# Sums of squares asked for later: the norms between the stages of a one-core encoder layer, and its last norm

## The chip, the cores and the metric

The kernel is one program on one core of a Trainium2 chip. The metric is the device time of one execution in microseconds (us). The core's engines are named as the profile names them: PE (TensorE, matrix products; PEld is its loading of weights), DVE (VectorE), ACT (ScalarE), POOL (GpSimd) and SP (SyncE, whose queue issues most of the loads from HBM). Each engine works through its own instructions in order and waits on semaphores for what the others produce.

## The reference

One layer of a streaming encoder on 1024 prompt frames and 32 sample frames, 1056 tokens in all, of 1024 channels. Each sub-layer stands between two norms, one of its input and one of its output:

```
def rms_norm(x, g):
    xf = x.astype(jnp.float32)
    y = xf * lax.rsqrt(jnp.mean(xf * xf, axis=-1, keepdims=True) + EPS) * g.astype(jnp.float32)
    return y.astype(x.dtype)
...
    mix = (jax.nn.sigmoid(ga) * (oa @ w_br_a) + jax.nn.sigmoid(gb) * (ob @ w_br_b)) @ w_out
    x = x + rms_norm(mix, g_post_mix)
    f, conv_new = conv_ffn(rms_norm(x, g_pre_ffn), conv_s0, w_up, conv_w, conv_b, w_down)
    x = x + rms_norm(f, g_post_ffn)
    gate = jax.nn.sigmoid(rms_norm(x, g_pre_ple) @ w_ple_gate)
    x = x + rms_norm(gate * (pe @ w_ple), g_post_ple)
```

`conv_ffn` is a product with `w_up` (1024 to 2 x 2816), a causal convolution of width 3 over one half of it, a gelu, a product of the two halves, and a product with `w_down` (2816 to 1024). The change touches the norms behind `w_out`, in front of `w_up`, behind `w_down`, in front of `w_ple_gate`, and the last one.

## The kernel before

**Layout and products.** Channels lie on the 128 partitions, in 8 rows of 128; tokens lie along the free dimension. A value in fp32 is kept as a high half (rounded to fp32r by ACT) and a low half (value less high half, by DVE or POOL), and a product is three matmuls: high by high, weight high by low half, weight low by high half. In most of the program the tokens are cut into three parts of 352; in the last stages into a part of 528 ("one"), one of 528 ("two"), and "two" again into 264 ("three") and 264 ("four"). A "pair" is two of the 8 rows.

**What a norm needs.** The squares of the 8 rows are made by ACT, pair by pair, and added up on DVE into an accumulator with two rows; DVE folds the two rows into one, ACT and DVE cut it into a high half h and a low half l, and PE sums it over the partitions by two matmuls with a matrix of ones (two per 264 columns). That is what is called "the sums" here. ACT then takes Ln and Exp of it (behind a load of its table), DVE does one Newton step in three instructions, and the inverse norm is there.

**The order of the work.** PE, DVE and ACT run in an order written out by hand: the code is written in the order in which each engine is to run it, and a generator that makes one norm is advanced step by step between the products. POOL's instructions and the order in which SP issues the loads are chosen by a scheduler that simulates the kernel.

**The up stage.** `norm_steps` (L1099 to L1166) is the generator for one part of 352 tokens. Its steps are: total of the out product's squares; first sums, inverse norm; four joins (scale a pair by channel and token, L1130, add the residual, L1144, with the square of the pair before ahead of it); last square; total; nothing; second sums, inverse norm; four steps that scale a pair again, spill it to the buffer d_hn and make its high and low half (L1159, L1166): the operand of `w_up`. The third part's steps are laid between the products of `up_plain` (L1288): 18 products of 24 matmuls (128 x 352), the table UP_STEPS saying how many steps come after each of the first nine. The sums are L1112 and L1113. Behind these products comes the first unit of a Strassen scheme, `up_first`: its operands are read back from d_hn and differenced on DVE (`quarter_first`, L1334 to L1338, with halves L1329 and L1330), and its weights are differenced too (L1370, halves L1376 and L1377).

**The down stage.** 28 units of 66 matmuls (128 x 264; L1728) accumulate the product with `w_down`. After unit u the program issues, in this order: the split of the weights of unit u+1 (`split_weights`: high halves on ACT, L1656, low halves from u = 19 on POOL, L1657), the additions that take unit u-1 out of PSUM (`evac`), and what a table puts into slot u: squares (`h_square`, L1781, their additions L1789 and L1791), fold and halves (L1796, L1798, L1799), joins (L1839, with the store of y by POOL, L1840), operands of the gate product (`operand`, L1843). The table MID puts the sums (L1807) into the middle of a unit: behind the matmuls of index k of it, six matmuls to an index.

**The gate stage and the tail.** 24 tiles follow (L1728 too), eight for part one, eight for three, eight for four, in a planned order; the table `sched` hangs work behind each. 16 transfers reload gate weights on SP's queue during it (L1989, L1990), and two transfers (`y_load`, L2075) read back part four of y. The last norm of part three has the name f3, that of part four g4: `gains` (L2071) scales a pair by its channel factors on ACT, `final` scales a pair by channel and token on DVE (L1834) and adds it to y by a transfer. Behind the last tile come the sigmoid of the last row, the last sums (L2193), Ln and Exp (L1817, L1818), the Newton step (L1819 to L1821), and four times a product and an addition (L2200, L2201) with a store.

Of the kernel before, what the change touches and what calls it, by code (L numbers as in the profile page):

```python
# [14 lines left out]
AF = mybir.ActivationFunctionType  # L15
# [85 lines left out]
OUT_STEPS = (1, 1, 2, 2, 2, 1, 1, 2)  # L101
UP_STEPS = (1, 1, 2, 2, 2, 1, 1, 2, 3)
DOWN_DVE = (0, 1, 2, 3, 4, 5)
# [3 lines left out]
def emit(tc, a):  # L107
# [992 lines left out]
    def norm_steps(tmp, c, z, acc, g, resid, keep, g_next, dst, spill=None):  # L1100
# [39 lines left out]
        for i in range(KT // 2):  # L1140
            if i:
                squares(tmp, acc2, i - 1, zs[i - 1])
            times(i, g, rs)
            ve.tensor_tensor(zs[i], zs[i], res[i], op=ALU.add)  # L1144
            if len(res) < KT // 2:
                load(len(res))
            po.dma_start(both(keep, i), zs[i])
            yield
# [694 lines left out]
    def operand(i, s, rs, dst):  # L1843
        zz = scaled(i, s, G_PRE_PLE, rs)
        ac.activation(dst[0], zz, AF.Copy)
        ve.tensor_tensor(dst[1], zz, dst[0], op=ALU.subtract)

# [59 lines left out]
    for i, u in enumerate((21, 22, 22, 23)):  # L1907
        at(u, n_join, "r1", i, one)
        at(u, h_square, "a2", i, one)
    at(24, n_total, "r2", "a2")  # L1910
# [3 lines left out]
    for j in range(3):  # L1914
        at(25 + j, h_square, "a3", j, two)
    MID = {21: (0, lambda: n_sum("r1")), 25: (3, lambda: n_sum("r2"))}

# [226 lines left out]
    on(19, g_begin, "g4", 3, four)  # L2144
    on(20, gains, 1, four)
    on(20, final, "f1", 3, one)
    on(21, gains, 2, four)
    on(21, n_inv, "f3")
    on(21, g_sig, "g4", 0)
    on(21, g_pair, "g4", 0, four)  # L2150
    on(22, gains, 0, four)
    on(16, y_load, 0)
# [13 lines left out]
    def g_first():  # L2166
# [4 lines left out]
        settle(acc)  # L2171

    on(22, g_first)
    on(22, final, "f3", 0, three)
    for g, (part, n) in enumerate(plan):
# [16 lines left out]
    for i, t in enumerate([kv[x][:, j] for x in ("g4", "s7") for j in range(2)]):  # L2192
        pe.matmul(ps, onesM, t, start=(i == 0), stop=(i == 3))  # L2193
    ac.activation(z[:, 7, four], z[:, 7, four], AF.Copy, scale=col(G_POST_PLE + 7))
    for i in range(1, 4):
        final("f3", i, three)
    rs = inverse(ps, False)
    for i in range(4):
        zz = z[:, 2 * i : 2 * i + 2, four]
        ve.tensor_tensor(zz, zz, rs.unsqueeze(1).to_broadcast([P, 2, HC]), op=ALU.mult)  # L2200
        ve.tensor_tensor(zz, zz, kv["y", i], op=ALU.add)  # L2201
        (dma, ac)[i % 2].dma_start(rows2(a["y"], i, four), zz)
# [89 lines left out]
```

## Time and profile before

| | us |
|---|---|
| median of 3 runs | 1921.74 |
| lowest and highest of them | 1918.62, 1922.12 |
| the profiled execution's own time | 1919.71 |
| its span, first to last instruction | 1918.0 |
| PE busy in it | 1886.7 (98%) |
| DVE busy | 1260.8 (66%) |
| ACT busy | 907.9 (47%) |
| POOL busy | 458.5 (24%) |

The mean granted clock of TensorE was 0.995. Of the profiled execution's own time, 1.71 us lie outside the span. Where the change lies: the products of `up_plain`, with the third part's norm among them, run from about 1107 to 1183 us of the span, `up_first` begins there, the down units run from 1577 to 1805, the gate tiles from 1805 to 1901.5, the tail from there to 1918.

How the rows are to be read: a row of the timeline has the start, the duration, the engine, the line, the operation, out <- in, the shape and the count of instructions that were taken together, and, in brackets, how long the engine was idle before and what released it. The recorded durations of matmuls overlap: two that follow each other at full rate start 0.12 us apart with 264 columns and 0.16 us apart with 352.

### The profile page before, as it was taken

Reading aid. Unit: us, or ns where it says so; the run is one execution under the profiler, and the core shown is the slowest. Engines: PE = TensorE matmul, PEld = TensorE weight load, DVE = VectorE, ACT = ScalarE, POOL = GpSimd, SP = SyncE. Lnnn points to the kernel's source line nnn. Section 1 sums busy time; section 2 is a strip of 40 time slices with the busy share of each in tenths; the row PEclk is TensorE's granted clock in tenths of the full one; section 3 lists DMA queues with packets and bytes.
Section 4 is the critical chain, followed back from the end, with each engine's and each line's share of the span. In section 5 each row is a group of like instructions: output and inputs, shape, how many; then the busy total and the mean of one; then the engine's idle time right before and its main releaser. Section 6 shows DMA issues by size and latency. Waiting matters only on the chain.

```text
span 1918.0 us, 34182 instructions
## 1 busy us (share of the span) xinstructions
PE 1886.7 (98%) x13364; PEld 1855.4 (97%) x13364; DVE 1260.8 (66%) x2521; ACT 907.9 (47%) x1668; POOL 458.5 (24%) x568
## 2 busy tenths in 40 slices
PE   9999999999999999999999999999999999999997
PEld 8999999999999999999999989999999999999996
DVE  6556556458486385775663787977777776546777
ACT  7456455444372452753334454433333344444545
POOL 2312232332232121222220212322222222115312
PEclk9999999999999999999999999999999999999999
DMA  7334346434445322337884446643443448656677
GB/s 273 120 97 136 114 125 161 119 132 123 108 133 141 104 68 74 112 121 261 309 274 143 148 144 219 198 148 126 153 131 131 136 161 299 193 183 200 200 248 152
DMA packets 106733, 307.77 MB, mean 160 GB/s; under 512 B 13188, under 2 KB 35276, under 8 KB 106444
## 3 DMA queue, kind: packets, MB, share of 16 engines
q1 hardware_dynamic: 80444, 217.64, 34.4%
q0 software_dynamic: 25296, 87.04, 15.3%
q8 instruction: 105, 1.72, 0.4%
q10 hardware_dynamic: 832, 0.90, 0.1%
q14 instruction: 56, 0.46, 0.1%
HBM read 217.79 MB, written 107.60 MB: 170 GB/s over the span
## 4 chain that ended last, share of the span: by engine, by line
PE 83%; DVE 10%; ACT 5%; issue 1%; DMA 1%; SPq 0%; ACTq 0%; DVEq 0%
PE mm L225 13%; PE mm L227 13%; PE mm L226 13%; PE c L1728 11%; PE two L1469 6%; PE two L1467 6%; PE two L1468 6%; PE aux L1728 2%; PE one L593 2%; PE one L551 2%; DVE z L1130 1%; PE two L535 1%; PE two L853 1%; PE one L911 1%; PE two L536 1%
## 5 line engine op out<-in xcount | busy, mean ns | idle before, releaser
L225 PE MATMUL mm<-xh,whi 128*128 128x352 f32 (+2 forms) x1248 | 412.3, 330 | 0.0
L227 PE MATMUL mm<-xh,wlo 128*128 128x352 f32 (+2 forms) x1248 | 409.9, 328 | 0.0
L226 PE MATMUL mm<-xl,whi 128*128 128x352 f32 (+2 forms) x1248 | 408.6, 327 | 0.0
L205 POOL TENSOR_TENSOR wlo<-raw,whi 128x512 fp32r<-128x512 f32 x128 | 187.7, 1470 | 661.3 <-ACT whi L204 657.4
L225 PEld LDWEIGHTS mm<-xh,whi 128*128 128x128 f32 x1248 | 235.2, 188 | 2.1 <-DVE ev L455 0.6
L226 PEld LDWEIGHTS mm<-xl,whi 128*128 128x128 f32 x1248 | 235.0, 188 | 1.5 <-issue 0.7
L227 PEld LDWEIGHTS mm<-xh,wlo 128*128 128x128 f32 x1248 | 234.5, 188 | 1.0
L1469 PE MATMUL two<-mh,wlo 128*128 128x264 f32 x576 | 162.8, 284 | 0.0
L1468 PE MATMUL two<-ml,whi 128*128 128x264 f32 x576 | 162.4, 283 | 0.0
L1467 PE MATMUL two<-mh,whi 128*128 128x264 f32 x576 | 161.1, 284 | 0.7 <-ACT whi L1457 0.7
L204 ACT ACTIVATE whi<-raw 128x512 fp32r<-128x512 f32 x136 | 84.2, 626 | 117.4 <-PE mm L226 88.4
L1728 PE MATMUL c<-mh,whi 128*128 128x264 f32 x396 | 112.4, 284 | 0.0
L1728 PE MATMUL c<-mh,wlo 128*128 128x264 f32 x396 | 112.2, 283 | 0.0
L1728 PE MATMUL c<-ml,whi 128*128 128x264 f32 x396 | 112.2, 283 | 0.0
L1468 PEld LDWEIGHTS two<-ml,whi 128*128 128x128 f32 x576 | 108.3, 188 | 0.0
L1469 PEld LDWEIGHTS two<-mh,wlo 128*128 128x128 f32 x576 | 108.3, 188 | 0.0
L1467 PEld LDWEIGHTS two<-mh,whi 128*128 128x128 f32 x576 | 107.3, 188 | 0.9 <-ACT whi L1457 0.9
L455 DVE TENSOR_TENSOR ev<-mm,rstd 128x352 f32<-128x352 f32 x120 | 61.6, 518 | 65.9 <-PE mm L227 65.3
L1457 ACT ACTIVATE whi<-ws 128x512 fp32r<-128x512 f32 x72 | 45.4, 632 | 99.9 <-PE two L1468 68.9
L555 DVE TENSOR_TENSOR pt<-one,pt 128x128 fp32r<-128x128 f32 (+3 forms) x96 | 46.3, 499 | 52.7 <-ACT pt L554 52.5
L225 PE MATMUL mm<-mh,ahi 128*128 128x352 f32 x240 | 78.1, 325 | 0.0
L226 PE MATMUL mm<-ml,ahi 128*128 128x352 f32 x240 | 78.0, 325 | 0.0
(575 smaller groups left out, 5435.1 us busy)
## 6 DMA issues: line engine op xcount, KB each, us to landing
raw<-in_w_in SPq DMA_DIRECT2D x52, 512.0 KB, 3.6
uraw<-d_b POOLq DMA_DIRECT2D x33, 528.0 KB, 5.0
raw<-in_w_up SPq DMA_DIRECT2D x26, 512.0 KB, 3.6
d_b<-av POOLq DMA_DIRECT2D x44, 264.0 KB, 2.7
d_s<-in_w_down POOLq DMA_DIRECT2D x16, 704.0 KB, 8.3
draw<-d_s SPq DMA_DIRECT2D x16, 704.0 KB, 4.2
hn<-d_b POOLq DMA_DIRECT2D x40, 264.0 KB, 3.7
d_b<-hn POOLq DMA_DIRECT2D x40, 264.0 KB, 2.5
```

What stands on the lines that cost most here:

```text
L204: ac.activation(hi[-1][:, d], raw[:, b], AF.Copy)
L205: eng.tensor_tensor(lo[-1][:, d], raw[:, b], hi[-1][:, d], op=ALU.subtract)
L225: pe.matmul(ps, h, xh(kt), start=(first and i == 0), stop=False)
L226: pe.matmul(ps, h, xl(kt), start=False, stop=False)
L227: pe.matmul(ps, l, xh(kt), start=False, stop=(last and i == n - 1))
L455: return lambda ps, s: ve.tensor_tensor(t[:, s], ps, rstd(s), op=ALU.mult)
L555: ve.tensor_tensor(out[1], tv, out[0], op=ALU.subtract)
L1457: ac.activation(h, x, AF.Copy)
L1467: pe.matmul(ps[:, j, :HC], w[0][:, k], x[0][:, k, s], start=st, stop=False, skip_group_check=True)
L1468: pe.matmul(ps[:, j, :HC], w[0][:, k], x[1][:, k, s], start=False, stop=False, skip_group_check=True)
L1469: pe.matmul(ps[:, j, :HC], w[1][:, k], x[0][:, k, s], start=False, stop=sp_, skip_group_check=True)
L1728: pe.matmul(ps, w, x, start=st, stop=sp_, skip_group_check=True)
```

## The change

Five edits, no instruction more or less.

1. **UP_STEPS** becomes (1, 0, 2, 2, 2, 2, 0, 3, 3) from (1, 1, 2, 2, 2, 1, 1, 2, 3): the third part's first sums stand behind product 2 instead of product 1, the second sums behind product 7 instead of product 6, and the joins between them a little later too.
2. **`norm_steps`**, for all three parts: the addition of a pair's squares is issued behind the next pair's scaling and residual addition instead of ahead of it.
3. **`operand`**: the low half of a pair is issued behind the scaling of the next pair.
4. **The down table**: the square of part one's last pair moves from slot 23 to slot 24, so behind the split of unit 25's weights, and the sums in unit 25 from behind k = 3 to behind k = 9.
5. **The last norm**: `gains` of pairs 1 and 2 of part four move behind the inverse norm f3; `final` of part three's pair 0 moves ahead of `g_first` and that of pair 1 joins it in slot 22, ahead of the last tile; the channel factor of row 7 moves behind the Ln and Exp of the last norm.

```
-UP_STEPS = (1, 1, 2, 2, 2, 1, 1, 2, 3)
+UP_STEPS = (1, 0, 2, 2, 2, 2, 0, 3, 3)
...
         for i in range(KT // 2):
-            if i:
-                squares(tmp, acc2, i - 1, zs[i - 1])
+            add = squares(tmp, acc2, i - 1, zs[i - 1], True) if i else None
             times(i, g, rs)
             ve.tensor_tensor(zs[i], zs[i], res[i], op=ALU.add)
+            if add:
+                add()
...
     def operand(i, s, rs, dst):
         zz = scaled(i, s, G_PRE_PLE, rs)
         ac.activation(dst[0], zz, AF.Copy)
-        ve.tensor_tensor(dst[1], zz, dst[0], op=ALU.subtract)
+        low_halves()
+        behind.append((dst[1], zz, dst[0]))
+        if i == 3:
+            low_halves()
+
+    behind = []
+
+    def low_halves():
+        while behind:
+            ve.tensor_tensor(*behind.pop(), op=ALU.subtract)
...
     for i, u in enumerate((21, 22, 22, 23)):
         at(u, n_join, "r1", i, one)
-        at(u, h_square, "a2", i, one)
+        at(u + i // 3, h_square, "a2", i, one)
...
-    MID = {21: (0, lambda: n_sum("r1")), 25: (3, lambda: n_sum("r2"))}
+    MID = {21: (0, lambda: n_sum("r1")), 25: (9, lambda: n_sum("r2"))}
...
-    on(20, gains, 1, four)
     on(20, final, "f1", 3, one)
-    on(21, gains, 2, four)
     on(21, n_inv, "f3")
     on(21, g_sig, "g4", 0)
+    on(21, gains, 1, four)
     on(21, g_pair, "g4", 0, four)
+    on(21, gains, 2, four)
     on(22, gains, 0, four)
...
+    on(22, final, "f3", 0, three)
     on(22, g_first)
-    on(22, final, "f3", 0, three)
+    on(22, final, "f3", 1, three)
...
-    ac.activation(z[:, 7, four], z[:, 7, four], AF.Copy, scale=col(G_POST_PLE + 7))
-    for i in range(1, 4):
+    for i in range(2, 4):
         final("f3", i, three)
     rs = inverse(ps, False)
+    ac.activation(z[:, 7, four], z[:, 7, four], AF.Copy, scale=col(G_POST_PLE + 7))
```

Line numbers of the changed kernel are one lower than those of the kernel before between L1141 and L1145, one higher behind that, and up to eleven higher behind L1843.

What that does to each engine's order stands in the next rows. In them a name with a number is one buffer of the program; in the first pair, PE, mm and one are PSUM banks, mh and ml the operand's halves, whi and wlo the weights' halves, y the halves h and l of the third part's total. PE in the up stage, before, the end of product 1 and what follows:

```order
L227 MATMUL mm_12095<-mh_10218,wlo_11940 128x352
L1112 MATMUL one_12121<-y_1899_12074,onesDr_75 128x352
L1113 MATMUL one_12121<-y_1900_12075,onesDr_75 128x352
L225 MATMUL mm_12133<-mh_10218,whi_11899 128x352
L226 MATMUL mm_12133<-ml_10219,whi_11899 128x352
```

And now, product 1's end, product 2's first rows and, 24 matmuls on, its end:

```order
L227 MATMUL mm_12095<-mh_10218,wlo_11940 128x352
L225 MATMUL mm_12121<-mh_10218,whi_11899 128x352
L226 MATMUL mm_12121<-ml_10219,whi_11899 128x352
...
L227 MATMUL mm_12121<-mh_10218,wlo_11904 128x352
L1112 MATMUL one_12147<-y_1899_12074,onesDr_75 128x352
L1113 MATMUL one_12147<-y_1900_12075,onesDr_75 128x352
L225 MATMUL mm_12174<-mh_10218,whi_11935 128x352
```

The same two sums are asked for one product, 24 matmuls, later. DVE between the third part's two norms, before (z the values, rs the inverse norm, res the residual, sq the squares, accn their accumulator, alo the low half of weights):

```order
L1086 SCALAR_TENSOR_TENSOR accn_12158<-sq_12204,accn_12158 128x704
L1130 SCALAR_TENSOR_TENSOR z_11699<-z_11699,vec_70,rs_12120 128x352 x2
L1144 TENSOR_TENSOR z_11699<-z_11699,res_12069 128x704
L1088 TENSOR_TENSOR accn_12158<-accn_12158,sq_12211 128x704
L1130 SCALAR_TENSOR_TENSOR z_11699<-z_11699,vec_70,rs_12120 128x352 x2
L1144 TENSOR_TENSOR z_11699<-z_11699,res_12071 128x704
L1088 TENSOR_TENSOR accn_12158<-accn_12158,sq_12248 128x704
L1095 TENSOR_TENSOR accn_12158<-accn_12158 128x352
L1107 TENSOR_TENSOR y_1926_12253<-accn_12158,y_1925_12252 128x352
```

And now:

```order
L1143 TENSOR_TENSOR z_11699<-z_11699,res_12069 128x704
L1086 SCALAR_TENSOR_TENSOR accn_12158<-sq_12204,accn_12158 128x704
L1130 SCALAR_TENSOR_TENSOR z_11699<-z_11699,vec_70,rs_12146 128x352 x2
L1143 TENSOR_TENSOR z_11699<-z_11699,res_12071 128x704
L1088 TENSOR_TENSOR accn_12158<-accn_12158,sq_12241 128x704
L1088 TENSOR_TENSOR accn_12158<-accn_12158,sq_12248 128x704
L1060 TENSOR_TENSOR alo_12254<-raw_12251,ahi_12253 128x512
L1060 TENSOR_TENSOR alo_12258<-raw_12251,ahi_12257 128x512
L1095 TENSOR_TENSOR accn_12158<-accn_12158 128x352
```

The first two additions of squares now stand behind a pair's scaling and residual, and two weight halves stand between the last of them and the fold. ACT in the down stage, the slots 23 and 24, before (mh the operand, dhi the high halves of unit 25's weights, pr the square, y the half h of the total):

```order
L1646 ACTIVATE mh_10218<-uraw_19551 128x528
L1781 ACTIVATE pr_19660<-z_17592 128x1056
L1656 ACTIVATE dhi_19731<-draw_19635 128x512
L1656 ACTIVATE dhi_19735<-draw_19635 128x512
L1656 ACTIVATE dhi_19739<-draw_19635 128x384
L1798 ACTIVATE y_2802_19747<-acc_19465 128x528
```

And now:

```order
L1647 ACTIVATE mh_10218<-uraw_19551 128x528
L1657 ACTIVATE dhi_19728<-draw_19635 128x512
L1657 ACTIVATE dhi_19732<-draw_19635 128x512
L1657 ACTIVATE dhi_19736<-draw_19635 128x384
L1782 ACTIVATE pr_19742<-z_17592 128x1056
L1799 ACTIVATE y_2802_19747<-acc_19465 128x528
```

The square stands behind the three weight halves. The scheduler, which orders SP's queue anew, also puts the first read-back of y (pr<-out_y) ahead of the 16 reloads of gate weights (mh and ml<-d_g) where it stood behind them. SP, before and then now:

```order
L2013 DMA uraw_20672<-d_pl_87 128x2x528
L1990 DMA ml_10219<-d_g_10214 128x512
L1989 DMA mh_10218<-d_g_10214 128x512 x2
L1990 DMA ml_10219<-d_g_10214 128x512
L1989 DMA mh_10218<-d_g_10214 128x512
```

```order
L2023 DMA uraw_20672<-d_pl_87 128x2x528
L2085 DMA pr_2926_20945<-out_y 128x4x264
L1999 DMA mh_10218<-d_g_10214 128x512
L2000 DMA ml_10219<-d_g_10214 128x512
L1999 DMA mh_10218<-d_g_10214 128x512
```

All 16 reloads now stand behind a transfer that reads what POOL's stores of y have written. Elsewhere on this queue, some loads in the stretch from `up_plain` to `up_first` change places: a quarter's first read of d_hn comes ahead of the quarter before's second one, and two loads of `w_up` come ahead of the last two reads of d_hn.

## The prediction

> **What bounds the kernel now.** I read the busy shares first, then PE's waits, then its timeline around them.
>
> ```profile
> PE 1886.7 (98%) x13364; PEld 1855.4 (97%) x13364; DVE 1260.8 (66%) x2521; ACT 907.9 (47%) x1668; POOL 458.5 (24%) x568
> ```
>
> PE is busy 98% of the span. No matmul is removed, so what can be won is idle time of PE, and the ends of the program where PE has nothing to do. The longest of the waits that the change can touch is this group:
>
> ```profile
> PE one L1112 <- ACT y L1106: 3.6, 2, 2.0
> ```
>
> Its columns are the total, the count and the longest: the third part's two sums wait 3.6 us for the half h of the total. The timeline of PE shows what lies around each of them:
>
> ```profile
> 1114.99 0.32 PE L227 MATMUL mm<-mh,wlo 128*128 128x352 f32 x1
> 1116.83 0.43 PE L1112 MATMUL one<-y,onesDr 128*128 128x352 f32 x1 [1.52 <-ACT y L1106]
> ...
> 1136.65 0.32 PE L227 MATMUL mm<-mh,alo 128*128 128x352 f32 x1
> 1139.02 0.43 PE L1112 MATMUL one<-y,onesDr 128*128 128x352 f32 x1 [2.05 <-ACT y L1106]
> 1139.58 0.43 PE L1113 MATMUL one<-y,onesDr 128*128 128x352 f32 x1
> ```
>
> At full rate matmuls start 0.16 us apart here. The first sums start 1116.83 - 1115.15 = 1.68 late, the second ones 1139.02 - 1136.81 = 2.21, and the second matmul of a pair follows 1139.58 - 1139.02 = 0.56 behind the first, 0.40 more than at full rate: 2.08 and 2.61 us. Behind these the clock falls, as the stretches show (length, then busy time with counts of PE, PEld, DVE, ACT, POOL, then the granted clock, DMA share, GB/s):
>
> ```profile
> 1113.30:1116.71 3.41, 2.01 (x13) 1.72 (x11) 2.91 (x5) 2.07 (x4) 0.72 (x1) 1.00 0.74 267
> 1137.19:1140.60 3.41, 1.45 (x7) 1.21 (x8) 2.81 (x5) 2.12 (x5) 0.00 (x0) 1.00 0.29 106
> 1140.60:1144.02 3.42, 3.42 (x14) 3.42 (x13) 1.15 (x3) 3.36 (x7) 0.00 (x0) 0.50 0.56 153
> 1184.00:1208.00 24.00, 20.78 (x155) 19.08 (x154) 22.39 (x28) 11.45 (x16) 9.30 (x14) 1.00 0.59 187
> 1208.00:1740.00 532.00, 532.00 (x4381) 531.97 (x4380) 375.75 (x557) 220.90 (x313) 125.88 (x240) 1.00 0.51 168
> ```
>
> In the third row the clock is 0.50. Half of 3.42 us is 1.7 us lost; by the count, 14 matmuls (those that reach over its edges among them) where 3.42 / 0.16 = 21.4 would start, it is 7.4 x 0.16 = 1.2. I take 1.6, nearer to the clock, since the count errs by its edges. The last two rows matter for what a gain upstream becomes: from 1184 to 1208 DVE, 22.39 of 24 us busy, is the tighter engine and PE idles 3.2 us; from 1208 to 1740 PE has no idle time at all, so whatever shift is left at 1208 reaches the down stage whole.
>
> **The up stage (edits 1 and 2).** One product is 24 x 0.16 = 3.84 us. Before, h of the first total comes 1.68 us after PE asks; one product later it is there. The same for the second. On PE alone the two edits remove 2.08 + 2.61 + 1.6 = 6.3 us. Edit 2 costs no instruction; it takes DVE's waits for the square out, of which this is one:
>
> ```profile
> 1133.26 0.89 DVE L1088 TENSOR_TENSOR accn<-accn,sq 128x704 f32<-128x704 f32 x1 [0.86 <-ACT sq L1081]
> 1136.99 0.89 DVE L1088 TENSOR_TENSOR accn<-accn,sq 128x704 f32<-128x704 f32 x1 [0.92 <-ACT sq L1081]
> 1139.00 0.53 DVE L1107 TENSOR_TENSOR y<-accn,y 128x352 fp32r<-128x352 f32 x1 [0.56 <-ACT y L1106]
> 1145.82 2.06 DVE L1130 SCALAR_TENSOR_TENSOR z<-z,vec,rstd 128x352 f32<-128x352 f32 x4
> ```
>
> The third part's chain gains 0.86 + 0.92 there and about 1.2 from the part before, which has the same two waits (an estimate: the same 1.8, of which ACT's own queue ahead of the Ln keeps a third); two weight halves of 128x512 that now stand ahead of the fold (0.68 us each by L1377 below) take as much back. So l is ready near 1139.53 - 1.8 = 1137.7, while PE, 2.08 - 0.4 earlier and one product further, asks at 1136.81 - 1.7 + 3.84 = 1139.0: covered by about 1 us. (The 0.4 is the price of the missing cover: product 2 now starts at 1115.15 and its operand's last low halves, 1.6 earlier than before, come about that much late.) With no wait there the clock should hold, and the final scaling starts near 1142.8, 3.0 earlier than in the fourth row.
>
> PE's 6.3 us are worth that only if what follows moves as much. It does not quite:
>
> ```profile
> 1158.45 0.71 DVE L1334 TENSOR_TENSOR hx<-hx 128x528 f32<-128x528 f32 x1 [5.23 <-DMA hx<-d_hn]
> 1161.79 0.71 DVE L1330 TENSOR_TENSOR t1l<-hx,t1h 128x528 fp32r<-128x528 f32 x1 [1.14 <-ACT t1h L1329]
> 1165.64 0.71 DVE L1330 TENSOR_TENSOR t1l<-hn,t1h 128x528 fp32r<-128x528 f32 x1 [0.42 <-ACT t1h L1329]
> 1175.78 0.71 DVE L1336 TENSOR_TENSOR hn<-hn,hn 128x528 f32<-128x528 f32 x1 [3.80 <-DMA hn<-d_hn]
> 1186.96 0.68 DVE L1377 TENSOR_TENSOR wlo<-raw,whi 128x512 fp32r<-128x512 f32 x1
> 1187.69 0.39 PE L1391 MATMUL two<-mh,wlo 128*128 128x264 f32 x1 [0.94 <-DVE wlo L1377]
> ```
>
> The spills, and with them the first read of d_hn, come 3.0 earlier. The waits of 1.14 and 0.42 for t1h are ACT standing behind a PSUM copy that waits for PE; PE being 6.3 earlier, they go: 3.0 + 1.14 + 0.42 = 4.6, about 4.7. The reads that end at 1175.78 are let go by DVE's own earlier steps and move with them. So wlo is 4.7 earlier, PE 6.3, and the wait of 0.94 grows to about 2.5: **-4.7 us** leave this stage. Bounds: -6.3 if the chain moves as PE does, -3.0 if only the first term passes; I take the middle because each of its terms has a row. The reordered loads on SP come into gaps of this chain; I give them nothing, and if one blocks, its price is a part of the lower bound.
>
> **A rule against it.** A 2.05 us wait was enough to halve the clock, when PE was busy 1.45 of the 3.41 us before; 2.01 of 3.41 was not. The wait of 2.5 that I expect at L1391 could do the same. The Trainium skill, "TensorE: Matmul & The Clock Gate", section "HAM oscillation", asks only that PE-idle gaps stay under about 3.4 us, so by it neither wait should cost any clock; the row of 0.50 disagrees with that for a gap of 2.05, and the measurement decides. By the rule the stage's PE term would be 4.7 instead of 6.3, which the chain's 4.7 already equals.
>
> **The down stage (edit 4).** The four waits of unit 25:
>
> ```profile
> 1778.01 0.39 PE L1728 MATMUL c<-mh,dhi 128*128 128x264 f32 x1 [0.44 <-ACT dhi L1656]
> 1779.37 0.39 PE L1728 MATMUL c<-mh,dlo 128*128 128x264 f32 x1 [0.85 <-POOL dlo L1657]
> ...
> 1782.87 0.39 PE L1807 MATMUL aux<-y,onesDr 128*128 128x264 f32 x1 [0.57 <-ACT y L1798]
> 1783.62 0.63 PE L1807 MATMUL aux<-y,onesDr 128*128 128x264 f32 x3 [0.36 <-DVE y L1799]
> ```
>
> Against 0.12 a start they cost 0.60, 1.01, 0.73 and 0.63 us: 2.97. What makes the first two late:
>
> ```profile
> 1776.35 1.09 ACT L1781 ACTIVATE pr<-z 128x1056 f32<-128x1056 f32 x1 [5.69 <-DVE z L1839]
> 1777.34 1.55 ACT L1656 ACTIVATE dhi<-draw 128x512 fp32r<-128x512 f32 x3
> 1778.04 4.96 POOL L1657 TENSOR_TENSOR dlo<-draw,dhi 128x512 fp32r<-128x512 f32 x3 [0.77 <-ACT dhi L1656]
> 1782.85 0.72 DVE L1799 TENSOR_TENSOR y<-acc,y 128x528 fp32r<-128x528 f32 x1 [0.71 <-ACT y L1798]
> ```
>
> The square held ACT 5.69 us for a join, and the weight halves stood behind it. With the halves first, dhi can start when ACT comes free, at 1776.35 - 5.69 = 1770.7, and dlo is done by about 1771.5 + 5 = 1776.5, ahead of both needs. The square keeps its time, its total is ready near 1783.5, and the sums are asked for six indices, 36 x 0.12 = 4.4 us, later: 1782.15 less the 1.6 of the first two waits, plus 4.4, is 1784.9. Margin 1.4 us. So **-3.0 us**. Bounds: 0 (the total comes as much later as the question) and -3.4 (the join at the stage's end moves too).
>
> **The gate stage.** Edit 3 changes nothing that PE waits for in the rows of before. The side effect on SP's queue does:
>
> ```profile
> 1847.02 0.72 POOL L1840 DMA_DIRECT2D out_y<-z  x1 [15.19 <-DVE z L1839]
> 1847.62 0.32 SPq L1990 DMA_DIRECT2D ml<-d_g  x1
> ml<-d_g SPq DMA_DIRECT2D x8, 256.0 KB, 5.2
> out_y<-z POOLq DMA_DIRECT2D x8, 264.0 KB, 5.2
> 1861.67 0.28 PE L1728 MATMUL c<-mh 128*128 128x264 f32 x1
> ```
>
> The second row is the first of the 16 reloads; the third and fourth say that a reload and a store of y land 5.2 us after their issue (median); the fifth is the first use of reloaded weights. The read-back ahead of them must wait for the store of 1847.02 to land, near 1852.2: the first reload goes out 4.6 us late, and with the four of the first tile half a us apart and 5.2 us each, the weights are there by 1859.5, 2 us before their use. Later ones have lost at most 4.6 us of the queue's time, which they partly make up. **+0.3 us**, bounds 0 and +2.
>
> **The tail (edit 5).** Behind PE's last tile DVE and ACT set the end.
>
> ```profile
> 1892.87 1.72 ACT L2071 ACTIVATE z<-z,vec 128x264 f32<-128x264 f32 x4
> 1902.70 0.37 ACT L2159 ACTIVATE raw<-c 128x264 f32<-128x264 f32 x1
> 1904.38 0.51 ACT L2194 ACTIVATE z<-z,vec 128x264 f32<-128x264 f32 x1
> 1903.94 2.50 DVE L1834 SCALAR_TENSOR_TENSOR z<-z,vec,rs 128x264 f32<-128x264 f32 x6
> 1906.37 0.42 DVE L1819 TENSOR_TENSOR y<-y 128x264 f32<-128x264 f32 x1
> ```
>
> The Newton step at 1906.37 stood behind six scalings of 0.42 us. Four are left: 0.83 us less. ACT's four channel factors (1.72 us) no longer hold the inverse norm f3, which brings the last sigmoid (1902.70) about 0.6 forward, and the factor of row 7 (0.51) leaves Ln's way. Newton's start then lies near 1905.1: **-1.3 us**. Bounds: -0.6 (the sigmoid's shift alone) and -1.7 (two scalings plus the 0.51 plus part of the shift).
>
> **The sum.** -4.7 - 3.0 + 0.3 - 1.3 = -8.7 us. The profiled execution took 1919.71, 2.03 below the median of the three runs; 1911.0 there, 1913.0 against the median.
>
> **Rivals.** (a) All of PE's gain comes through: -6.3 - 3.0 - 1.3 = -10.6, 1911.1. For it: DVE waits on reads that could come sooner (5.23, 3.80); against it: 22.39 busy of 24. (b) The up stage gives everything back at L1391, because the reads of d_hn at 1175.78 are set by SP's queue and not by the chain: -3.0 + 0.3 - 1.3 = -4.0, 1917.7. For it: the 3.80 wait on a DMA; against it: those buffers are freed by DVE. (c) The total of unit 25 is late again, since POOL's low halves now run beside DVE's additions: half of -3.0 is lost, 1914.5. (d) The wait at L1391 halves the clock for one stretch: +1.6, 1914.6. Against it: PE waits there for DVE anyway. (e) The moves change the order but the waits only move elsewhere, no gain at all: 1921.7. (f) The other side: the 16 reloads now hang on DVE's join, for which POOL sat idle 15.19 us. Once the join comes more than 2 us later than now, every us more is a us of PE's; from 11 us late the kernel is slower than before, and with 15 it takes 1921.74 - 9.0 + 13 = 1925.7. For it: the read-back did not stand ahead of any weight before; against it: nothing in the change makes the join late.
>
> **How the numbers follow.** The forecast 0.48, (a) 0.10, (b) 0.14, (c) 0.09, (d) 0.04, (e) 0.10, (f) 0.05. A difference under 0.2%, 3.8 us, cannot be told from none. The forecast, (a), (c) and (d) are faster: 0.71; (b) lies on the border (4.0), half of it faster: 0.78. Same: half of (b) and (e), 0.17. Slower: 0.05. The range runs from 1909.0, the sum of the far bounds (-6.3 - 3.4 - 1.7 = -11.4, 1910.3) less 1.3 for the spread of the runs shown, to 1919.0, past (b); outside are (e), (f) and little else.
>
> **What would show it.** Right: no wait at L1112 of the third part, no stretch at 0.50 behind it, a wait of 2 to 3 us at L1391 where 0.94 stood, the four waits of unit 25 gone, the gate tiles starting 7 to 8 us earlier, Newton's step 1.3 us sooner after the last tile. Wrong: a wait in the new places of the sums, an L1391 wait of 5 us or more (b), a wait for mh or ml in the gate tiles (f), or a clock under 1.00 between 1177 and 1208.

## The result, and the profile after

The changed kernel takes 1907.95 us (median of 5 runs, 1907.14 to 1908.89), the kernel before 1919.13 beside it (5 runs, 1917.42 to 1922.12): a ratio of 0.9938, interval 0.9925 to 0.9952, about 12 us. On another chip it was 1908.79 against 1918.88, ratio 0.9948 (0.9936 to 0.9961). So it is faster, as forecast, but by more: 11 us between the medians where the sum gave 8.7, and 1907.95 lies 1.05 us under the range, which began at 1909.0. Of all runs below, one execution of e11_wlo took 3065.86 us at a mean granted clock of 0.555 and is left out of that run's numbers.

The profiled execution of the changed kernel took 1908.14, its span is 1906.4. Its busy shares, and of its list of PE's waits the one group that answers to those shown before:

```profile
PE 1882.6 (99%) x13364; PEld 1853.7 (97%) x13364; DVE 1262.2 (66%) x2521; ACT 908.1 (48%) x1668; POOL 460.1 (24%) x568
```

```profile
PE two L1392 <- DVE wlo L1378: 1.3, 2, 1.1
```

L1112, 3.6 us before, is no longer in the list, nor are dhi, dlo and the acc of the last sums. DVE's timeline has the final scaling and the weight half that PE waits for:

```profile
1142.95 2.07 DVE L1130 SCALAR_TENSOR_TENSOR z<-z,vec,rstd 128x352 f32<-128x352 f32 x4
...
1181.22 0.69 DVE L1378 TENSOR_TENSOR wlo<-raw,whi 128x512 fp32r<-128x512 f32 x1
```

PE's timeline has the two sums of the third part in step with what precedes them, and the stretches around the second pair keep the clock at 1.00 (columns as before):

```profile
1119.41 0.33 PE L227 MATMUL mm<-mh,wlo 128*128 128x352 f32 x1
1119.58 0.32 PE L1112 MATMUL one<-y,onesDr 128*128 128x352 f32 x1
...
1138.92 0.32 PE L227 MATMUL mm<-mh,alo 128*128 128x352 f32 x1
1139.07 0.32 PE L1112 MATMUL one<-y,onesDr 128*128 128x352 f32 x1
...
1181.96 0.39 PE L1392 MATMUL two<-mh,wlo 128*128 128x264 f32 x1 [1.08 <-DVE wlo L1378]
```

```profile
1133.60:1137.00 3.40, 3.40 (x23) 3.40 (x22) 2.94 (x5) 2.19 (x5) 0.61 (x1) 1.00 0.29 106
1137.00:1140.40 3.40, 3.40 (x24) 3.40 (x23) 1.82 (x3) 3.37 (x7) 0.00 (x0) 1.00 0.55 160
```

The last row of the timeline above is the surprise: PE's wait in the first Strassen unit did not grow from 0.94 to 2.5, it is 1.08.

Where the time went is seen best by the same matmul in each trace. The matmuls without the sums come in the same order in all these kernels, so the distance between two of them can be compared. The marks are, by the clock of the kernel before, the last matmul of product 1 (1114.99), the first of product 8 (1145.24), one behind the first Strassen unit (1205.89), one in unit 24 (1770.6), one at the start of unit 26 (1788.9), one in the second gate tile (1816.4), the last tile's last matmul (1901.26), and the end of the span. Distances in us:

| kernel | third norm | first Strassen | to unit 24 | unit 25 | to the gate | gate | tail |
|---|---|---|---|---|---|---|---|
| before | 30.26 | 60.64 | 564.74 | 18.31 | 27.43 | 84.89 | 16.75 |
| changed | 23.99 | 60.48 | 564.68 | 15.45 | 27.70 | 84.28 | 14.45 |
| difference | -6.27 | -0.16 | -0.06 | -2.86 | +0.27 | -0.61 | -2.30 |
| edits 1 and 2 | 23.90 | 60.84 | 564.75 | 18.31 | 27.42 | 84.93 | 17.02 |
| edit 1 | 27.26 | 61.85 | 564.61 | 18.31 | 27.42 | 84.94 | 17.11 |
| edit 2 | 25.05 | 60.77 | 564.76 | 18.31 | 27.44 | 84.94 | 17.26 |
| edit 4 | 28.69 | 59.08 | 564.61 | 15.47 | 31.81 | 84.91 | 17.03 |
| edit 3 | 30.18 | 61.38 | 564.59 | 18.32 | 27.12 | 84.27 | 16.67 |
| edits 3 and 4 | 28.72 | 60.22 | 564.76 | 15.47 | 27.66 | 84.27 | 16.82 |
| edit 5 | 28.70 | 59.96 | 564.68 | 18.33 | 27.44 | 84.90 | 14.40 |
| changed, less edit 3 | 23.97 | 60.93 | 564.63 | 15.45 | 32.99 | 84.94 | 14.43 |

The differences of the first pair add up to -12.0; another +0.4 arose ahead of the first mark, where of the change only edit 2 lies, in the norms of the first two parts (without a stretch at half clock on the way, the first mark is at 1113.8 to 1116.0 in the traces with edit 2 and at 1115.0 to 1116.2 in those without). The change is visible in four columns, and each gain crosses the 565 us of the Strassen units whole, as forecast.

### The profile page after: what moved, and what is told of

The parts are those of the page before. It is cut to its first block, busy times and chain, and to the rows that moved or that the text cites. A ratio compares the mean times of both kernels' runs of the same rounds, so it can differ in the third digit from the quotient of the medians.

```text
span 1906.4 us, 34185 instructions
## 1 busy us (share of the span) xinstructions
PE 1882.6 (99%) x13364; PEld 1853.7 (97%) x13364; DVE 1262.2 (66%) x2521; ACT 908.1 (48%) x1668; POOL 460.1 (24%) x568
## 4 chain that ended last, share of the span: by engine, by line
PE 81%; DVE 10%; ACT 4%; issue 3%; DMA 2%; POOL 0%; SPq 0%; DVEq 0%; ACTq 0%; POOLq 0%
PE mm L225 13%; PE mm L226 13%; PE mm L227 13%; PE c L1729 11%; PE two L1470 6%; PE two L1468 6%; PE two L1469 6%; PE aux L1729 2%; PE one L593 2%; PE one L551 2%; PE two L535 1%; PE two L853 1%; PE one L911 1%; PE two L536 1%; DVE z L1835 1%
```

## The experiments

Each run is timed against the kernel before on its own chip. The theory at the start: edits 1 and 2 take PE's whole loss in the up stage, edit 4 the waits of unit 25, edit 5 the tail, each by itself.

**The up stage.** First edits 1 and 2 together, then each alone.

```
 e1_up:    UP_STEPS = (1, 0, 2, 2, 2, 2, 0, 3, 3), additions of squares later
 e2_defer: only the additions of squares later
 e3_steps: only UP_STEPS
```

> Edits 1 and 2 alone (the table UP_STEPS and the later additions of squares; the rest as before). Theory A, that the two edits take all of PE's loss in the up stage and that the chain to the first Strassen unit moves as much: 6.0 to 6.5 us faster, both waits at the third part's sums and the stretch at clock 0.50 gone, the wait of PE at the weight's low half in the first Strassen unit (0.94 before) about 1.1. Theory B, that the chain's move needs the other edits (through the order of SP's loads, which each edit changes): 4 to 5 us faster, with 2 us or more of wait there.

> Edit 2 alone: the additions of squares later, the sums where they stood. Theory A: the chain gains 1.6 us by the first sums and about 3.3 by the second, so the first wait falls from 1.7 to about 0.2 and the second from 2.2 to about 1, the clock holds at 1.00, and 4 to 5 us are gained. If the clock halves after a wait of about 1 us too, 2.5 to 3.5.

> Edit 1 alone: the sums one product later, the additions of squares where they stood. Theory A: the first wait goes from the sums to the operand of the next product (2 us for a low half, nothing gained there), the second sums wait 0.3 or less and the clock holds, 4 us for PE, but the chain behind it is only 1 to 3 us earlier, so the wait in the first Strassen unit grows to 2 us or more and 2 to 3.5 us are gained. If the two edits are independent, this run and that of edit 2 add up to that of both; by theory A they add up to more than it.

Measured: both 0.9972 (0.9961 to 0.9984), 1914.93 against 1920.23; edit 2 alone 0.9984 (0.9976 to 0.9993), 1917.64; edit 1 alone 0.9992 (0.9983 to 1.0001), 1918.73. So 5.4, 3.1 and 1.5 us: they nearly add up, with edit 2 the larger, and neither theory's number for both is excluded by the interval (3.1 to 7.5 us). The trace of both speaks for theory A in what it says of the other edits: the two columns add up to 84.74 where the changed kernel has 84.47, and PE's wait at the weight's low half is 1.4 us, not 2 or more:

```profile
PE two L1392 <- DVE wlo L1378: 1.8, 3, 1.4
```

So the chain moves without edits 3 to 5. Edit 2 alone gains less than the 4 to 5 expected (interval 1.3 to 4.6), and edit 1 alone less than the 2 to 3.5, an amount that the interval cannot tell from none. With edit 1 alone the wait goes where it was expected to go, to the next product's operand, and then to the first Strassen unit, because DVE's chain is no earlier (PE's timeline of that run):

```profile
1120.40 0.43 PE L226 MATMUL mm<-ml,whi 128*128 128x352 f32 x1 [1.82 <-DVE ml L1159]
...
1187.38 0.45 PE L1391 MATMUL two<-mh,wlo 128*128 128x264 f32 x1 [2.30 <-DVE wlo L1377]
```

Behind that wait of 2.30 the granted clock was 0.50 for one stretch, from 1187.57 to 1190.98: what rival (d) of the prediction had described for the changed kernel.

With edit 2 alone the second sums wait 0.31 us, less than the 1 us expected, and no stretch at half clock follows:

```profile
1138.86 0.43 PE L1112 MATMUL one<-y,onesDr 128*128 128x352 f32 x1 [0.31 <-ACT y L1106]
```

**The down stage.** Edit 4 alone:

> Edit 4 alone: the square behind the weight halves and the sums six indices later in unit 25. Its order of SP's loads in the up stage has the quarter's read swapped as in the changed kernel, with the norms as before, so it also shows the swap alone. Theory A: the four waits of unit 25 gone, 3.0 us there, and the up stage as before within 0.4 us. If the swap is what moves the chain: PE's wait of 0.94 in the first Strassen unit gone and up to 1 us more.

It is not faster: 1.0009 (1.0000 to 1.0017), 1922.19 against 1920.23, which neither theory had. Nor does it show the swap of the reads that I expected of it: in its trace SP issues the loads of the up stage in the order of the kernel before. In the table it wins 2.84 us in unit 25 and loses 4.38 on the way to the gate. Its PE timeline there:

```profile
1804.51 0.39 PE L1728 MATMUL c<-mh,whi 128*128 128x264 f32 x1 [0.34 <-ACT mh L1845]
1805.80 0.39 PE L1728 MATMUL c<-ml,whi 128*128 128x264 f32 x1 [0.90 <-DVE ml L1846]
1811.54 0.39 PE L1807 MATMUL aux<-y,onesDr 128*128 128x264 f32 x1 [1.97 <-ACT y L1798]
```

PE comes earlier, but the operand of the gate product, and the sums behind it, do not. What makes the operand earlier in the changed kernel was tried by taking edit 3 out of it, by edits 3 and 4 together, and by edit 3 alone:

```
 e8_no_oper:   the changed kernel, each low half of operand() at once again
 e9_oper_down: edits 3 and 4
 e15_oper:     edit 3
```

> The changed kernel without edit 3 (low half of each pair at once again); this also puts the first read-back of y behind the 16 reloads again. As my prediction has it (edit 3 worth nothing, the read-back 0 to 2): 0 to 2 us faster than the changed kernel. Rival, from the run of edit 4 alone, where the gate tiles lost 4.3 us at their start to the operand's high and low half and to the sums: 3 to 4.5 us slower than the changed kernel, all of it between 1795 and 1815 us.

> Edits 3 and 4 together, the rest as before. If edit 3 is the cover that edit 4 needs (theory from the runs so far): the four waits of unit 25 gone and none at the start of the gate tiles, 3 us faster in the profile, where edit 4 alone gave back 4.3 us; some 3 to 5 us faster than edit 4 alone and 2 to 4 faster than before. If the loss of edit 4 alone had another cause than the operand's order: the waits for mh, ml and y at the start of the gate tiles stay and it is no faster than before.

> Edit 3 alone; its order of SP's loads also has the first read-back of y ahead of the 16 reloads of gate weights, the rest as before. By the theory that edit 3 only matters once PE comes earlier: same time as before within 1 us, low halves of the operand done about 3 us sooner, nobody waiting for them. It also shows the read-back alone: 0 to 2 us slower in the gate tiles if the reloads come late (my prediction: 0.3), with waits for mh or ml from the twelfth tile on; none if they have time enough.

Without edit 3 the changed kernel takes 1914.47 instead of 1908.79 on the same chip, 5.7 us more, and more than the 3 to 4.5 of the rival; edits 3 and 4 are 0.9981 (0.9973 to 0.9990); edit 3 alone is 0.9994 (0.9985 to 1.0003). So 4 alone loses, 3 alone does nothing that can be told, and together they win 3.7 us (1.9 to 5.2): edit 3 is the cover that edit 4 needs. The mechanism is in DVE's rows, first of edit 4 alone, then of the changed kernel:

```profile
1797.45 1.44 DVE L1834 SCALAR_TENSOR_TENSOR z<-z,vec,rs 128x528 f32<-128x528 f32 x2
1800.05 1.26 DVE L1846 TENSOR_TENSOR ml<-z,mh 128x1056 fp32r<-128x1056 f32 x1 [1.15 <-ACT mh L1845]
...
1804.49 1.26 DVE L1846 TENSOR_TENSOR ml<-z,mh 128x1056 fp32r<-128x1056 f32 x1 [1.21 <-ACT mh L1845]
```

```profile
1785.08 5.04 DVE L1835 SCALAR_TENSOR_TENSOR z<-z,vec,rs 128x528 f32<-128x528 f32 x4
1790.04 1.25 DVE L1856 TENSOR_TENSOR ml<-z,mh 128x1056 fp32r<-128x1056 f32 x1
...
1795.71 2.55 DVE L1856 TENSOR_TENSOR ml<-z,mh 128x1056 fp32r<-128x1056 f32 x2
```

For each pair DVE waits some 1.15 us for ACT's high half before it can make the low one; with edit 3 the next pair's scaling fills that time, and the last low half is done at 1798.3, while without it the four waits add up to about 4.7 us. In the kernel before the same waits stood there and cost nothing, since unit 25's 3 us kept PE back. Taking edit 3 out also draws a stretch at half clock, behind the wait for the sums (stretches of that run, columns as before):

```profile
1804.36:1807.77 3.41, 1.45 (x13) 1.23 (x11) 2.56 (x4) 1.27 (x3) 0.00 (x0) 1.00 0.51 154
1807.78:1811.19 3.41, 3.25 (x13) 2.95 (x14) 0.65 (x1) 3.37 (x4) 0.00 (x0) 0.50 0.01 2
```

The run of the changed kernel itself beside these, on the second chip:

> The changed kernel itself, beside the next three on one chip, as what they are compared with. 10 to 13 us faster than the kernel before; by the traces so far the gain is 6.2 in the up stage, 3 in the down stage, 2 behind the last tile, and the rest of the spread between executions is single stretches of 3.4 us at half clock (1.7 us each) that fall in some executions and not in others.

It was 10.1 us faster by the medians (1908.79 against 1918.88).

How near the total of unit 25 is to being late again was asked by moving the sums back to k = 3 in the changed kernel (`MID = {..., 25: (3, ...)}`):

> The changed kernel with unit 25's sums back behind k = 3 (the square still in slot 24). If the total is ready when my prediction had it (near 1783.5 by the clock of the kernel before, 1.4 us ahead of the question behind k = 9): the sums wait 4.4 - 1.4 = 3 us, and the kernel is 3 us slower than the changed one, or 1.5 to 2 more where that wait halves the clock.

The sums wait 3.88 us, not 3, and the clock halves behind that. The run takes 1914.62, ratio 0.9974 (0.9965 to 0.9983); unit 25's column goes from 15.45 to 21.06, which is 3.9 of wait and 1.7 of clock.

```profile
1778.74 0.52 PE L1808 MATMUL aux<-y,onesDr 128*128 128x264 f32 x1 [3.88 <-ACT y L1799]
```

So of the 4.4 us by which edit 4 moves the question only some 0.3 is left over, not 1.4. The second half l is not even ready in time: in the changed kernel the second of the four sums starts 0.41 us behind the first instead of 0.12. The total is later than forecast: with POOL's low halves at 1765.74 (5.47 us for three) DVE's two scalings ahead of the join take 3.24 us at 1768.54 where two of the same shape took 1.43 at 1791.21, with POOL idle.

```profile
1765.74 5.47 POOL L1658 TENSOR_TENSOR dlo<-draw,dhi 128x512 fp32r<-128x512 f32 x3
```

```profile
1768.54 3.24 DVE L1835 SCALAR_TENSOR_TENSOR z<-z,vec,rs 128x528 f32<-128x528 f32 x2
...
1791.21 1.43 DVE L1835 SCALAR_TENSOR_TENSOR z<-z,vec,rs 128x528 f32<-128x528 f32 x2
```

The Trainium skill, "SBUF — State Buffer", section "Who interferes with whom", says that a DVE instruction with two inputs from SBUF contends with a GpSimd instruction that reads SBUF; the two rows agree with it, at 2.3 times the duration.

**The order of the reads, and PE's wait in the first Strassen unit.** By the traces, edits 1 to 4 each change the order of SP's loads a little, edit 5 does not; with edit 1 or edit 2, and so in the changed kernel, quarter 3's first read of d_hn comes ahead of quarter 2's second. In the first run the reads are held in the order of the program, in the next two that wait is attacked directly:

```
 e12_noswap: quarter_load's two dma_start held in program order
 e11_wlo:    the gated product of the first plain unit (L1257) behind the
             unit's first four weight sums and halves
 e16_la12:   the low half of the unit's second weight right behind the first's
 e19_both:   e16_la12 and e12_noswap
```

> The changed kernel with the reads of d_hn for the four quarters held in the order of the program, so quarter 2's second read stands ahead of quarter 3's first again, as in the kernel before. As my prediction has it (the order of the loads worth nothing): same as the changed kernel, wait of PE at the first Strassen unit's weight 1.1 as there. Rival, from the run of edit 4 alone, where that swap came with unchanged norms and took the wait of 0.94 away: the wait is 2 to 2.5 us and the kernel 1 to 2 us slower than the changed one, which is the 4.7 us of my sum for the up stage.

> The changed kernel with the gated product of the first plain unit (3 us of DVE) issued behind the four weight halves and sums of the first Strassen unit instead of ahead of them. If PE's wait of 1.1 us there is all that the order costs: wait gone and 0.5 to 1.1 us faster than the changed kernel. If DVE's whole work in that stretch sets the pace: the wait moves to the next weight halves and nothing is gained, within 0.3 us.

> The changed kernel with the low half of the first Strassen unit's second weight issued right behind that of its first, in the gap in which DVE waits 0.98 us for a gelu. If that wait of PE (1.1) is what the stretch costs: wait gone, 0.7 to 1.1 us less from the end of the plain products to the end of that unit. If DVE's whole work sets the pace there: the wait goes to the next weights, 0 to 0.4 less.

> The same, and the reads of d_hn for the quarters in program order. With both, DVE's chain is up to 1.5 us earlier than in the changed kernel: 1 to 1.5 us less in that stretch if PE waits for this chain alone; no better than the run before if the order of the reads is worth nothing.

e12_noswap takes 1908.11 against 1908.79 of the changed kernel on its chip, ratio 0.9948 (0.9934 to 0.9962): no difference that can be told, so the order of the reads is worth nothing that these runs show; PE's longest wait for that weight is 0.6 us there, not 2 to 2.5. e11_wlo takes 1912.66 (0.9965, 0.9953 to 0.9977), 3.9 us more, which neither expectation had: in its trace PE waits 3.0 us for a later weight half, and the clock is 0.50 for the 6.8 us from 1191.45. e16_la12 takes 1908.91, 0.9953 (0.9939 to 0.9966), e19_both 1909.17, 0.9950 (0.9938 to 0.9963): the wait at the second weight is gone, and a wait of twice its size stands one weight further on (PE's row of e16_la12):

```profile
1188.20 0.39 PE L1392 MATMUL two<-t1h,wlo 128*128 128x264 f32 x1 [2.02 <-DVE wlo L1378]
```

In both runs the clock is 0.50 for one stretch behind that wait. So the wait moved on, as the second theory had it, that DVE's whole work sets the pace there and not one late weight half; how much of the result is that stretch of clock is not separated. I had taken the run of edit 4 for one with the swap of the reads, and its wait of 0.94, which was gone (59.08 in the second column of the table), for the swap's effect. It has the order of before, and so have the runs of the scalings alone and of the factors alone below, with 59.26 and 58.85 there, and edit 3 alone with 61.38: this column differs that much between executions of the same code in this stretch. None of these versions beats the changed kernel.

**The tail.** Edit 5 alone, then its scalings alone and its channel factors alone:

> Edit 5 alone. From the profile of the changed kernel: Newton's first step 3.5 us behind the start of the last tile's last matmul instead of 5.1, so 1.6 us faster; 2.3 if the 0.7 by which the last store was shorter there belongs to the edit, 1.6 if that was this one execution. My prediction had 1.3.

> Of edit 5 only the scalings of part three (pair 0 ahead of the last row's sigmoid, pair 1 with it), the channel factors where they were. By my sum: 0.8 us less to Newton's step, which then waits for Ln behind the factor of row 7, so 0.8 to 0.9; and, if the shorter end of the last stores comes from part three's stores being issued sooner, 0.9 less behind DVE's last instruction here too.

> Of edit 5 only the channel factors (pairs 1 and 2 behind the inverse norm, row 7 behind Ln and Exp), the scalings where they were. By my sum: Newton's step stays behind six scalings on DVE, and only the sigmoid comes earlier: 0.6 us less or nothing; the end behind DVE's last instruction as before (4.6 to 5.2).

Edit 5 is 0.9989 (0.9980 to 0.9998), 1917.36 against 1919.91; the scalings 0.9996 (0.9988 to 1.0005), the channel factors 1.0000 (0.9991 to 1.0009). The times cannot tell the two parts from no change, the traces can: the factors win more than the 0.6 expected, the scalings less than the 0.8. In us from the last tile's last matmul to Newton's first step, and from DVE's last instruction to the end:

| kernel | to Newton's step | behind DVE's last |
|---|---|---|
| before | 5.11 | 4.72 |
| channel factors alone | 4.16 | 5.07 |
| scalings alone | 4.46 | 4.14 |
| edit 5 | 3.49 | 3.97 |
| changed | 3.48 | 4.03 |

The eight profiled executions without the moved scalings have 4.64 to 5.23 in the second column, the ten with them 3.86 to 4.46. The stores show why: issues in the tail, with KB each and median us to landing, of the kernel before and of the scalings alone:

```profile
out_y<-z POOLq DMA_DIRECT2D x4, 264.0 KB, 5.7
out_y<-z SPq DMA_DIRECT2D x2, 264.0 KB, 3.7
```

```profile
out_y<-z POOLq DMA_DIRECT2D x4, 264.0 KB, 4.7
out_y<-z SPq DMA_DIRECT2D x2, 264.0 KB, 3.1
```

Part three's four adding stores on POOL's queue are still landing when part four's are issued; with the scalings moved, all four are issued sooner, the first by 2.4 us and the others by 1.2 to 1.6, counted from the last tile's last matmul, and the two of part four on SP's queue land 0.6 us earlier after their issue. That they share the DMA engines is argued from these rows, not tried by itself.

## Why the prediction was right and wrong

**The base.** I set the sum against the median of the three runs shown, 1921.74, adding 2.03 to the profiled execution's 1919.71. Medians of more runs of the same kernel were 1919.13, 1918.88, 1919.05, 1920.23 and 1919.91 (5, 16, 21, 30 and 33 runs): the profiled execution was typical, the median of three was high. Against 1919.13, the median beside the changed kernel, this step alone is 2.6 of the 5 us between 1913.0 and 1907.95, and more than what put the result outside the range. The rest lies in the terms: by the traces the four stages give -4.8, -2.6, -0.6 and -2.3, together -10.3, where the sum had -4.7, -3.0, +0.3 and -1.3.

**The up stage: -4.7, measured -5.4 by the runs (3.1 to 7.5) and -4.8 by the traces.** The mechanism was right: both sums in step, the clock kept, the final scaling at 1142.95 (forecast 1142.8). The step that failed is "So wlo is 4.7 earlier, PE 6.3, and the wait of 0.94 grows to about 2.5". DVE's chain came 5.7 earlier, not 4.7 (wlo at 1181.22 against 1186.96): the two holds for t1h went as forecast (1.14 and 0.42). Most of the rest came from reads of d_hn that landed: DVE's waits for them add up to 10.0 us before and 8.8 in the changed kernel. The sum held them fixed, which the row of 5.23 does not show: the same read ends a wait of 4.46 in the changed kernel and of 6.08 in the run of edits 3 and 4. Why they differ stays open.

```profile
1154.82 0.71 DVE L1335 TENSOR_TENSOR hx<-hx 128x528 f32<-128x528 f32 x1 [4.46 <-DMA hx<-d_hn]
```

```profile
1160.15 0.71 DVE L1334 TENSOR_TENSOR hx<-hx 128x528 f32<-128x528 f32 x1 [6.08 <-DMA hx<-d_hn]
```

Nor was the 1.6 us of clock a property of the kernel. Of seven profiled executions with the norms as before, four had the stretch at 0.50 at 1140, two had one from 1119.43 or 1122.25 instead, which shortened the second wait (their third norm takes 28.7), and the run of edit 4 had none, with a wait just as long:

```profile
1139.58 0.43 PE L1112 MATMUL one<-y,onesDr 128*128 128x352 f32 x1 [2.13 <-ACT y L1106]
```

```profile
1134.88:1138.29 3.41, 2.57 (x17) 2.28 (x15) 2.46 (x4) 0.79 (x1) 0.71 (x1) 1.00 0.23 82
1138.30:1141.71 3.41, 2.00 (x11) 1.76 (x12) 2.48 (x5) 2.66 (x6) 0.00 (x0) 1.00 0.25 91
```

These two rows are laid on that execution's own stretches of 3.41 us, counted on from the stretch at half clock at its start, which ended at 11.90 us. The wait falls on the border of two of them, each is busy 2.00 us or more, and the clock stays; in the kernel before it fell into one, busy 1.45, and the clock halved. The Trainium skill, "TensorE: Matmul & The Clock Gate", section "What's actually happening", says that the window is free-running and 3413 ns long, with which these stretches agree; that a whole idle window is needed for the clock to fall, as its table there has it, they do not show: half a window was enough. So the first two columns together, with the norms and the order of reads as before, are 87.8 to 91.6 over seven executions (mean 89.5), and 84.4 to 84.9 over five with edits 1 and 2 (mean 84.7): 4.8 us. My 4.7 was near that mean by luck, for a reason that did not hold.

**The down stage and edit 3: -3.0, measured -2.6.** The runs of edits 3 and 4 give -3.7, but that holds the gate stage's gain too; by the table unit 25 gains 2.86 of the 2.97 forecast, and 0.27 goes again on the way to the gate. The step that failed is the sentence that edit 3 "changes nothing that PE waits for in the rows of before". Those rows could not show it: the waits it removes were hidden behind the very 3 us that edit 4 takes away. I had costed it at nothing without naming the cover; without it the way to the gate gives back 4.4 us, and 5.3 where the clock halves too (32.99 against 27.70). By the same lack of care the margin of the sums was forecast at 1.4 and is 0.3: of rival (c), POOL beside DVE did happen, and just fitted.

**The gate stage: +0.3, measured -0.6.** The read-back does wait for the store of 1847.02 to land, as forecast. The failed step is the time, "near 1852.2": the store's old place and the median of 5.2 us. In the run of edit 3 alone DVE joins that pair sooner, POOL issues the store at 1844.94, and SP, which waits 4.0 us for it, sends the read-back 2.7 us behind the store (the changed kernel has the same 2.7). The first reload goes out at 1848.73, 1.1 us later than before and not 4.6, in an execution that enters the gate stage 1.0 us later. Nobody waited for a reload. The gain of 0.6 comes with edit 3: every row of the table that has it is at 84.27 or 84.28, the others at 84.89 to 84.94. By the same matmuls in both traces it is two short waits of PE, 0.28 us at 1870.6 and 0.31 at the sums of 1877.7 by the clock of the kernel before; both are gone where DVE is ahead. POOL's store, SP's wait for it and the two rows of SP's queue in the run of edit 3 alone:

```profile
1844.94 0.72 POOL L1840 DMA_DIRECT2D out_y<-z  x1 [13.31 <-DVE z L1839]
```

```profile
SPq L2084 <- DMA out_y<-z: 4.0, 1, 4.0
```

```profile
1847.65 0.38 SPq L2084 DMA_DIRECT2D pr<-out_y  x1
1848.73 0.33 SPq L1998 DMA_DIRECT2D mh<-d_g  x1
```

**The tail: -1.3, measured -2.3.** (Edit 5 alone has 2.35 in its trace and 2.1 by the ratio of its runs, 0.4 to 3.8.) To Newton's step it is 1.62: the scalings alone 0.65, the factors alone 0.95. The mis-sized term is the shift of the last row's sigmoid, which I had at about 0.6: it started 1.44 us behind the last tile's last matmul (1902.70 less 1901.26) and now starts 0.48 behind it (1892.46 less 1891.98), 0.96 sooner, and the factors alone bring all of that to Newton's step. In the changed kernel the step then waits for Exp, and Ln for PE's last sums:

```profile
1892.46 0.37 ACT L2169 ACTIVATE raw<-c 128x264 f32<-128x264 f32 x1
...
1894.59 0.39 ACT L1818 ACTIVATE y<-aux 128x264 f32<-128x264 f32 x1 [0.46 <-PE aux L2204]
```

The 0.7 to 0.9 behind DVE's last instruction was missing from the sum: I counted the moved scalings on DVE and not the stores that each of them releases.

**The rivals.** (a) has the nearest number, -10.6 against -10.1 to -11.9, but not its mechanism: the up stage gave 4.8 us by the traces and not 6.3, the gate and the tail gave more. (b), (e) and (f) did not occur. (d) did not in the changed kernel, whose wait at that place was 1.08; in the runs where PE waited 2.0 to 2.4 us in that unit (edit 1 alone, e16_la12, e19_both) the clock did halve for one stretch.

## What to carry to other kernels

Where two stalls of one engine lie one behind the other, the first hides the chain of the second: before a stall is taken out, the chain that is due next has to be walked at the earlier time, and an edit that shows no effect in the profile before may be what pays for another. With a moved instruction its stores move too, and here the end of the kernel came sooner with them. And a sum made against a profiled execution is better left at that execution than carried over to a median of three runs with a spread of 3.5 us.

## What the runs showed of the hardware that was not expected

A wait of PE of 2.0 to 2.1 us halves the granted clock for the next 3.41 us or not, by how it lies to the stretches of 3.41 us in which the clock is decided. In each of the 18 traces every stretch at 0.50 begins a whole number of times 3.413 us behind the end of the first one. PE's busy time was counted in every such stretch at a clock of 1.00, behind the program's start and ahead of the tail: those busy 1.69 us or less, half of 3.41, were all followed by one at 0.50 (eleven of them), those busy 2.1 or more never, and in between both are found. This does not hold outside these limits: at the program's start, stretches busy 2.25 to 2.29 us were followed by half clock in three traces, and in the run of edit 5 one at half clock, fully busy, was followed by a second.

A stretch costs up to 1.7 us, and probably makes up a good part of the spread between executions of the kernel before (1915.94 to 1923.29 in 33 runs): of these, the eight with a mean granted clock of 0.996 took 1918.46 us in the mean, the five with 0.994 took 1921.72. The changed kernel, without such a wait in its profiles, had runs from 1907.14 to 1909.39 on two chips.
